# Second attention of a two-layer trunk: its first projections and its first step issued earlier in the program

## The chip, the cores and the metric

The kernel runs on one core of one Trainium2 chip. The metric is the device time of one execution in microseconds (us). A core has five engines that run their own instruction queues in order: PE (TensorE, matrix multiplications and transposes), DVE (VectorE), ACT (ScalarE), POOL (GpSimd) and SP (SyncE, which here issues most of the DMA transfers). [...]

## The reference

Two layers over 1024 tokens of width 1024, each a token mixer and a gated MLP with a causal convolution of width 3. Layer 0 mixes with differential attention (8 heads), layer 1 with multi-head latent attention (16 heads). The change is about the seam between the input of layer 1's mixer and its heads:

```
proj = h @ w_in                                   # 1024 -> 384 + 256 + 32
c_q  = rms_norm(proj[..., :384], q_norm_g)
c_kv = rms_norm(proj[..., 384:640], kv_norm_g)
k_pe = apply_rope(proj[..., 640:], cos, sin)      # one rotary key, shared by all heads
q  = (c_q @ w_uq).reshape(b, s, 16, 64 + 32)      # q_nope, q_pe
kv = (c_kv @ w_ukv).reshape(b, s, 16, 64 + 64)    # k_nope, v
p  = masked_softmax((q_nope . k_nope + q_pe . k_pe) * scale, chunk mask)
out = (p @ v) @ w_o
```

All of it is in float32. A product of two float32 operands is made of three matmuls: each operand is split into a high part and the rest.

## The kernel before

**The latent input** (`mla_input`) loops over `i` = 0 to 9, with eight tiles of 128 tokens (`NT` = 8). Round `i` does `latents(i)` (48 matmuls into one of the two `S` accumulators, then two RMS norms), `turn(i - 1)` (six transposes, then the split into the high and low parts of `c_q` and `c_kv`), and `values(i - 2)` (12 matmuls, two copies by ACT, a DMA of the values to `v_d` in HBM; the first pair's values are also kept on chip by `own`). Round 5 turns the rotary key of tokens 0 to 511 (`rotary(0)`), round 8 that of tokens 512 to 1023 (`rotary(1)`, and `share(1, 1)`, which copies it to the second head's key tile).

**The heads** (`mla_heads`) go in pairs. A pair has six units: `k_unit(p, half)` (6 matmuls, the keys of both heads for one half of the tokens) and `q_unit(h, half)` (9 matmuls). `first()` runs the three units of pair 0 on tokens 0 to 511; before the change it stands in round 7, ahead of `latents(7)`.

**The steps** (`steps`): a head has four steps; each takes two blocks of 128 queries. Step `t` issues `scores(0)` (q times k, row maximum on DVE, exponential on ACT), the units that `units(t)` hands it, the `turn` (transposes of the probabilities, line 252) of step `t - 1`, `weigh(0)`, `scores(1)`, the rest of the units, the `product` with the values (lines 1726 and 1727) of step `t - 1`, and `weigh(1)`. The second attention's steps come in the order p = 1, 0, 3, 2, so its steps 0 and 1 use tokens 0 to 511 alone, and step 2 all of them. Step 0 gets pair 0's three units for tokens 512 to 1023. `prepare(t)` adds fetches and splits of weights and values: in step 0 the fetch of pair 1's weights (`fetch_w(1)`), in step 1 their split, in step 2 the fetch of pair 1's values from `v_d`, in step 4 their split. The differential attention's steps use the same function with its own units of 24 matmuls, into a single accumulator `u`.

**What sets the order.** The kernel says what depends on what; which instruction an engine takes next is fixed when the program is built, by a scheduler that runs through the program with estimated durations and gives each engine the ready instruction that stands first in the program's text order. So a place further up in the text is a higher priority, not a fixed time. Regions under `manual_schedule` keep the order as written; the seam of this change is in none of them. On the chip, every engine then works through its queue in that order.

**The memory** is cut into named places (`s`, `u`, `h` with a number), each used by one tile after another; a ring hands its places out in the order of the calls. `raw` is such a ring of two (`u14`, `u15`): weights from HBM and the values on their way to `v_d` take turns in it. `R.P` is the ring of probability tiles. The eight normalised input tiles of `mla_input` lie in `s4`, `s5`, `s13`, `s0`, `s1`, `s10`, `s11`, `s12`, and each place comes free when `latents` of its tile is done.

Of the kernel before, what the change touches and what calls it, by code (L numbers as in the profile page):

```python
# [17 lines left out]

P = 128
S = 1024  # L20
D = 1024
NT = S // P
KD = D // P
EPS = 1e-6
NEG = -3.0e38

DA_HEADS = 8
# [3 lines left out]
MLA_HEADS = 16  # L31
# [5 lines left out]
FFN = 2816  # L37
NF = FFN // P

# [17 lines left out]
class Trunk:  # L57
# [7 lines left out]
    def __init__(self, tc, ctx, a):  # L65
# [8 lines left out]
        for kind, count, size in (("s", 14, 2048), ("u", 16, 1024), ("h", 14, 512)):  # L74
            for i in range(count):
                self.at(f"{kind}{i}", [P, size])

# [23 lines left out]
    def cut(self, place, size=1024):  # L101

        tile = self.at(place, [P, 2048])
        return [tile[:, i : i + size] for i in range(0, 2048, size)]
# [173 lines left out]
            if n is not None:  # L278
                n -= 1

    def steps(self, attend, units, prepare, n):


        steps = []
        for t in range(n + 2):
            now = before = None
            u = []
            if t < n:
                now = attend(t)
                steps.append(now)  # L290
                prepare(t)
                u = units(t)
                now.scores(0)
            if 0 < t <= n:
                before = steps[t - 1]
            self.run(u, 1)
            if before:
                before.turn()
            if now:
                now.weigh(0)  # L300
                now.scores(1)
            self.run(u)
            if before:
                before.product()
            if now:
                now.weigh(1)
            if t >= 2:
                steps[t - 2].finish()


    def diff_attention(self, o_d, prefetch):
        nc, a = self.nc, self.a
# [5 lines left out]
        R = SimpleNamespace(  # L318
            k=self.ring("u0", "u1", "u2"), qh=self.ring("u3", "u4"), v=self.ring("u5", "u6", "u7"),
            P=self.ring("u8", "u9", "u10", "u11", "u12"), pT=self.ring("u13", "u14", "u15"),  # L320
            o=self.ring("h2", "h3"), fin=self.ring("h4", "h5", "h6", "h7"),
            rope=self.ring("h8", "h9", "h10", "h11"),
        )
# [5 lines left out]
        heads = [dict(q=[None, None], k=[None, None], v=[None, None]) for _ in range(DA_HEADS)]  # L329
# [20 lines left out]
        x, r = [], {}  # L350
# [183 lines left out]
                todo = [[(h, 1, 1)], [(h, 0, 1)], [(h, 2, 1)], []][p]  # L534
            return [unit(*u) for u in todo if u[0] < DA_HEADS]

        self.steps(lambda t: DaStep(self, R, *divmod(t, 4), heads, o_d), units, prepare, 4 * DA_HEADS)

    def da_unit(self, R, H, W, which, half, hd, tab):

# [793 lines left out]
    def mla_input(self, W, hts, turns, v_d, heads_of):  # L1334
# [14 lines left out]
        def latent_tiles(half):  # L1349
            for x, place in zip((cq, ckv), (("s2", "s3"), ("s6", "s7"))[half]):  # L1350
                pieces = self.at(place, [P, 4, 512], F32R)
                for part in range(2):
                    x[part].append(pieces[:, 2 * part : 2 * part + 2, :])
            for part in range(2):
                cq2[part].append(self.at(f"h{2 * half + part}", [P, 512], F32R))
# [7 lines left out]
        def latents(i):  # L1363
            acc = self.big()
            for k in range(KD):
                for b, m, kind in ((0, 384, "q"), (512, 288, "kv")):
                    wh, wl = where[kind, k]
                    self.mm3(acc[:, b : b + m], hts[i][:, 0, k, :], hts[i][:, 1, k, :], wh, wl, k == 0, k == KD - 1)
            nat = nats([P, 672])
            for b, m, off, gain in ((0, 384, 0, g[0]), (512, 256, 384, g[1])):  # L1370
                d = nat[:, off : off + m]
                r = self.rstd(acc[:, b : b + m], d, m)
                nc.vector.scalar_tensor_tensor(d, acc[:, b : b + m], r, gain, ALU.mult, ALU.mult)
            nc.scalar.copy(nat[:, 640:672], acc[:, 768:800])
            return nat

        def turn(i, nat):
            half = i // 4
            s = slice((i % 4) * P, (i % 4 + 1) * P)
            ps = self.bank()  # L1380
            for j in range(3):
                nc.tensor.transpose(ps[:, j * P : (j + 1) * P], nat[:, j * P : (j + 1) * P], self.ident)
            v = ps.rearrange("p (k s) -> p k s", s=P)
            for dst, src in ((cq, v[:, 0:2]), (cq2, v[:, 2])):
                h, l = (x[half][:, s] if dst is cq2 else x[half][:, :, s] for x in dst)
                self.hi(h, src)
                self.lo(l, src, h)
            ps = self.bank()
            for j in range(2):
                nc.tensor.transpose(ps[:, j * P : (j + 1) * P], nat[:, (3 + j) * P : (4 + j) * P], self.ident)  # L1390
            nc.tensor.transpose(ps[:MLA_ROPE, 256:384], nat[:, 640:672], self.ident)
            v = ps[:, :256].rearrange("p (k s) -> p k s", s=P)
            self.hi(ckv[0][half][:, :, s], v)
            self.lo(ckv[1][half][:, :, s], v, ckv[0][half][:, :, s])
            nc.scalar.copy(kp[half][:, s], ps[:MLA_ROPE, 256:384])

        def values(i):
            half = i // 4
            s = slice((i % 4) * P, (i % 4 + 1) * P)
            vs = self.raw([P, D])  # L1400
            for b, y in ((0, self.bank("u")), (512, self.bank())):
                for k in range(2):
                    ch, cl = (cT.kv(part, half, k)[:, s] for part in range(2))
                    self.mm3(y, ch, cl, late.wv[k][0][:, b : b + 512], late.wv[k][1][:, b : b + 512], k == 0, k == 1)
                if b == 0:
                    heads.own(i, y[:, :P])
                nc.scalar.copy(vs[:, b : b + 512], y)
            nc.sync.dma_start(v_d[:, :, i].rearrange("h p e -> p h e"), vs.rearrange("p (h e) -> p h e", e=P))

        def fetch_tab(half):  # L1410
            late.tab = [self.at(place, [MLA_ROPE, 512]) for place in ("h12", "h13")]
            for x in range(2):
                nc.sync.dma_start(late.tab[x], a["rope_k"][:, x, half * 512 : (half + 1) * 512])

        def rotary(half):
            r = self.rope(rope, kp[half], *late.tab, MLA_ROPE // 2, MLA_ROPE)
            t = nats([MLA_ROPE, 2, 512], F32R)
            self.hi(t[:, 0, :], r[:MLA_ROPE])
            self.lo(t[:, 1, :], r[:MLA_ROPE], t[:, 0, :], nc.gpsimd)
            heads.rotary(half, t)  # L1420
# [3 lines left out]
        for i in range(NT + 2):  # L1424
            if readies:
                readies.pop(0)()
            if i == NT - 1:
                heads.share(1, 0)
                heads.first()
            if i < NT:  # L1430
                nat[i] = latents(i)
                if turns:
                    turns.pop(0)()
            if i in (1, 5):
                latent_tiles(i // 4)
            if i == 1:

                late.wv = [self.split(f"s{4 + k}", self.fetch(a["mla_wuv"][k * P : (k + 1) * P, :], D)) for k in range(2)]
                heads = heads_of(cT)
            if i == 4:  # L1440
                fetch_tab(0)
            if 0 <= i - 1 < NT:
                turn(i - 1, nat.pop(i - 1))
            if i >= 2:
                values(i - 2)
            if i == 5:
                rotary(0)
                fetch_tab(1)
            if i == NT:
                rotary(1)  # L1450
                heads.share(1, 1)
        return heads

    def mla_heads(self, cT, v_d, o_d):
        nc, a = self.nc, self.a
        pairs = MLA_HEADS // 2
        heads = [dict() for _ in range(MLA_HEADS)]
        W, V, raws = {}, {}, {}
        w_places = [("u2", "u3"), ("u4", "u5")]
        v_ring, q_ring, t_ring = self.ring("s13", "s4"), self.ring("s1", "s10", "s5", "s9"), self.ring("h10", "h11", "h8")  # L1460
        k_places, kT = ["s0", "s11", "s12", "s8"], []
        cs = self.at("u13", [P, S])
        nc.sync.dma_start(cs, a["rope_q"])
        R = SimpleNamespace(
            P=self.ring("u6", "u7", "u8", "u9", "u12"), pT=self.ring("u0", "u1", "u10", "u11"), o=self.ring("h4", "h5", "h6", "h7"),
        )

        def fetch_w(p):
# [46 lines left out]
        def pair_units(p):  # L1515
            return [
                lambda: k_unit(p, 0), lambda: k_unit(p, 1),
                lambda: q_unit(2 * p, 0), lambda: q_unit(2 * p, 1),
                lambda: q_unit(2 * p + 1, 0), lambda: q_unit(2 * p + 1, 1),
            ]  # L1520
# [1 line left out]
        fetch_w(0)  # L1522
        split_w(0)

        def first():

            self.run([u() for u in pair_units(0)[::2]])

        def own(i, y):

# [49 lines left out]

        prefetch = []

        def rest(step):
            prefetch.append(step)
            self.steps(attend, units, prepare, 4 * MLA_HEADS)

        return SimpleNamespace(first=first, own=own, rotary=rotary, share=share, rest=rest)


class Step:  # L1590
# [431 lines left out]
```

## Time and profile before

| | |
|---|---|
| time, median of 3 runs | 2427.79 us (2427.32 to 2431.45) |
| the profiled execution's own time | 2430.68 us |
| its span from first to last instruction | 2428.9 us |
| PE busy | 2355.0 us of the span |
| DVE, ACT, POOL busy | 1916.0, 1305.3, 618.5 us |
| differential attention, head steps | from about 40 to 510 us |
| latent input | from about 1240 to 1335 us |
| second attention, head steps | from about 1326 to 1680 us |

Engine shares are averages over stages with different limits: the MLP stages (from 620 to 1000 us and from 1820 to 2200 us) have PE busy without a gap. A line such as `1347.25 1.05 ACT L127 CAST s<-u ... [1.46 <-DMA u<-v_d]` in a timeline says: start, duration, engine, line of the kernel, operation, output and input, and in brackets how long the engine had been idle and what it waited for.

### The profile page before, as it was taken

To read this page: it belongs to the slowest core of one execution; us is meant where nothing else is said; L and a number is where in the kernel's file an instruction comes from. 1 tells how busy PE (TensorE), PEld (TensorE's weight loads), DVE (VectorE), ACT (ScalarE), POOL (GpSimd) and SP (SyncE) were. 2 spreads that over 40 slices of the span, in tenths; PEclk is the share of its full clock that TensorE was granted. 3 is DMA by queue.
4 is the path that set the end of the run, shared out by engine and by line. 5 is a ranking of instruction groups with operands and counts; after the bars stand their busy time and mean duration, and the time that the engine had idled before them with its cause. 6 is when DMAs were issued, how large, how long until landed. Compare 5 with 4: busy or idle time off the path is not lost.

```text
span 2428.9 us, 32660 instructions
## 1 busy us (share of the span) xinstructions
PE 2355.0 (97%) x11936; PEld 1997.5 (82%) x11936; DVE 1916.0 (79%) x3111; ACT 1305.3 (54%) x2446; POOL 618.5 (25%) x489
## 2 busy tenths in 40 slices
PE   7999999999999999999999999999999999999998
PEld 6888787887888888878899788988878888887886
DVE  6667776857888888889964777887488888888997
ACT  5677777755444444444445777776244444444444
POOL 4545454424100000000041666665330000000001
PEclk9999999999999999999999999999999999999999
DMA  4111111223322222554221211114322222227502
GB/s 161 40 35 44 35 35 44 100 93 100 99 82 79 87 78 88 187 175 131 72 103 46 77 40 29 49 59 134 96 87 87 79 87 87 78 86 278 172 3 78
DMA packets 95792, 213.91 MB, mean 88 GB/s; under 512 B 8720, under 2 KB 33936, under 8 KB 95632
## 3 DMA queue, kind: packets, MB, share of 16 engines
q1 hardware_dynamic: 86448, 184.04, 23.1%
q10 hardware_dynamic: 9184, 27.79, 3.1%
q8 instruction: 94, 1.54, 0.3%
q14 instruction: 66, 0.54, 0.1%
HBM read 159.37 MB, written 52.43 MB: 87 GB/s over the span
## 4 chain that ended last, share of the span: by engine, by line
PE 82%; DVE 7%; ACT 5%; DMA 3%; issue 2%; POOL 1%; SPq 0%; DVEq 0%; POOLq 0%; ACTq 0%
PE S L119 13%; PE S L121 13%; PE S L120 13%; PE b L119 8%; PE b L120 8%; PE b L121 8%; PE u L119 4%; PE u L120 4%; PE u L121 4%; PE b L252 3%; DMA u<-g_d 2%; PE u L1727 1%; DVE s L130 1%; PE u L1726 1%; ACT s L127 1%
## 5 line engine op out<-in xcount | busy, mean ns | idle before, releaser
L167 POOL TENSOR_TENSOR st<-st,mhalf 128x1 f32<-128x1 f32 x56 | 36.6, 654 | 1314.1 <-DVE st L164 1305.5
L127 ACT CAST u<-h 128x512 fp32r<-128x512 f32 (+2 forms) x242 | 145.9, 619 | 297.4 <-DVE h L847 277.7
L119 PE MATMUL S<-s,u 128*128 128x512 f32 (+1 forms) x768 | 290.5, 378 | 7.6 <-ACT s L127 2.6
L121 PE MATMUL S<-s,u 128*128 128x512 f32 (+1 forms) x768 | 289.5, 377 | 0.1
L120 PE MATMUL S<-s,u 128*128 128x512 f32 (+1 forms) x768 | 289.4, 377 | 0.0
L119 PE MATMUL b<-s,u 128*128 128x512 f32 x588 | 231.0, 393 | 1.5 <-DVE u L130 0.8
L121 PE MATMUL b<-s,u 128*128 128x512 f32 x588 | 229.3, 390 | 0.0
L120 PE MATMUL b<-s,u 128*128 128x512 f32 x588 | 229.2, 390 | 0.0
L904 DVE SCALAR_TENSOR_TENSOR u<-u,conv,u 128x1023 f32<-128x1023 f32 (+1 forms) x176 | 225.8, 1283 | 1.4 <-ACT u L900 1.4
L149 POOL TENSOR_TENSOR u<-u,st 128x384 f32<-128x384 f32 (+7 forms) x160 | 169.7, 1068 | 151.0 <-DVE st L1712 106.7
L127 ACT CAST s<-u 128x512 fp32r<-128x512 f32 (+2 forms) x230 | 145.0, 666 | 108.2 <-PE u L121 35.8
L119 PE MATMUL u<-s,s 128*128 128x512 f32 (+1 forms) x440 | 178.5, 406 | 13.4 <-ACT h L556 7.0
L130 DVE TENSOR_TENSOR u<-b,u 128x512 fp32r<-128x512 f32 (+1 forms) x256 | 157.4, 629 | 29.4 <-ACT u L127 28.0
L119 PEld LDWEIGHTS S<-s,u 128*128 128x128 f32 x768 | 145.2, 189 | 35.1 <-ACT s L127 5.5
L121 PE MATMUL u<-s,s 128*128 128x512 f32 (+1 forms) x440 | 173.2, 394 | 0.0
L120 PE MATMUL u<-s,s 128*128 128x512 f32 (+1 forms) x440 | 172.8, 393 | 0.0
L121 PEld LDWEIGHTS S<-s,u 128*128 128x128 f32 x768 | 145.2, 189 | 26.6 <-DVE u L130 0.5
L120 PEld LDWEIGHTS S<-s,u 128*128 128x128 f32 x768 | 145.3, 189 | 26.1
L130 DVE TENSOR_TENSOR s<-u,s 128x512 fp32r<-128x512 f32 (+2 forms) x210 | 150.0, 746 | 12.4 <-ACT s L127 12.2
L127 ACT CAST u<-b 128x512 fp32r<-128x512 f32 (+1 forms) x256 | 133.2, 550 | 37.9 <-PE b L252 28.9
L907 ACT ACTIVATE u<-u 128x1024 f32<-128x1024 f32 x44 | 46.7, 1062 | 187.5 <-DVE u L904 187.5
L130 DVE TENSOR_TENSOR u<-h,u 128x512 fp32r<-128x512 f32 x164 | 112.7, 687 | 32.5 <-ACT u L127 31.5
(270 smaller groups left out, 6561.1 us busy)
## 6 DMA issues: line engine op xcount, KB each, us to landing
u<-in_ffn_up SPq DMA_DIRECT2D x88, 512.0 KB, 3.9
g_d<-u ACTq DMA_DIRECT2D x44, 512.0 KB, 2.6
u<-in_ffn_down SPq DMA_DIRECT2D x66, 256.0 KB, 4.8
u<-g_d SPq DMA_DIRECT2D x62, 256.0 KB, 4.4
s<-in_da_wqkv SPq DMA_DIRECT2D x23, 512.0 KB, 3.6
x_d<-u SPq DMA_DIRECT2D x16, 512.0 KB, 2.9
s<-x_d SPq DMA_DIRECT2D x8, 1024.0 KB, 10.8
u<-o_d SPq DMA_DIRECT2D x24, 256.0 KB, 2.9
```

The costliest lines, as they stand in the source:

```text
L119: mm(out, lh, rl, start=first, stop=False, skip_group_check=onto)
L120: mm(out, lh, rh, start=False, stop=False, skip_group_check=onto)
L121: mm(out, ll, rh, start=False, stop=last, skip_group_check=onto)
L127: self.nc.scalar.copy(out, src)
L130: (eng or self.nc.vector).tensor_sub(out, src, hi.bitcast(F32))
L149: self.nc.gpsimd.tensor_mul(x, x, s.to_broadcast(list(x.shape)))
L167: nc.gpsimd.tensor_tensor(r, s, self.mhalf, ALU.pow)
L252: self.nc.tensor.transpose(ps[:, j * P : (j + 1) * P], probs[t][:, k : k + P], self.ident)
L904: nc.vector.scalar_tensor_tensor(t[half][:, back:], u[half][:, : S - back], w, t[half][:, back:], ALU.mult, ALU.add)
L907: nc.scalar.activation(t[0], t[0], AF.Silu)
L1726: nc.tensor.matmul(o[:, c0:], v, al, start=kb == 0, stop=False)
L1727: nc.tensor.matmul(o[:, c0:], v, ah, start=False, stop=kb == 2 * p + 1)
```

## The change

- `first` takes the numbers of the units. Keys and the first head's queries of pair 0 (units 0 and 2, tokens 0 to 511) now stand in round 6, ahead of `latents(6)`; the second head's queries (unit 4) stay in round 7.
- `share(1, 0)` moves with them from round 7 to round 6.
- `steps` has become a generator that yields once a step. `early()` issues step 0 of the second attention at the end of round 8, so ahead of `values(7)`, and step 1 at the end of round 9, where it stood before.
- Buffers: the second head's queries go to `s11` and its keys to `s10`, before the other way round; the ring of probabilities starts at `u12` instead of `u6`.
- `steps` gets an option `apart`, set for the differential attention alone: where a step has two units, the first one is issued as a whole, its matmuls ahead of the turn of the step before; before the change its second half came behind `scores(1)`.

```diff
-    def steps(self, attend, units, prepare, n):
+    def steps(self, attend, units, prepare, n, apart=False):
...
-            self.run(u, 1)
+            alone = u[:-1] if apart else []
+            if alone:
+                u = u[-1:]
+            self.run(alone or u, 2 if alone else 1)
             if before:
                 before.turn()
+            self.run(alone)
             if now:
                 now.weigh(0)
                 now.scores(1)
...
+            yield
...
-        self.steps(lambda t: DaStep(self, R, *divmod(t, 4), heads, o_d), units, prepare, 4 * DA_HEADS)
+        self.run([self.steps(lambda t: DaStep(self, R, *divmod(t, 4), heads, o_d), units, prepare, 4 * DA_HEADS, True)])
...
+            if i == NT - 2:
+                heads.share(1, 0)
+                heads.first(0, 2)
             if i == NT - 1:
-                heads.share(1, 0)
-                heads.first()
+                heads.first(4)
...
+            if i >= 8:
+                heads.early()
...
-        v_ring, q_ring, t_ring = self.ring("s13", "s4"), self.ring("s1", "s10", "s5", "s9"), self.ring("h10", "h11", "h8")
-        k_places, kT = ["s0", "s11", "s12", "s8"], []
+        v_ring, q_ring, t_ring = self.ring("s13", "s4"), self.ring("s1", "s11", "s5", "s9"), self.ring("h10", "h11", "h8")
+        k_places, kT = ["s0", "s10", "s12", "s8"], []
...
-            P=self.ring("u6", "u7", "u8", "u9", "u12"), pT=self.ring("u0", "u1", "u10", "u11"), o=self.ring("h4", "h5", "h6", "h7"),
+            P=self.ring("u12", "u6", "u7", "u8", "u9"), pT=self.ring("u0", "u1", "u10", "u11"), o=self.ring("h4", "h5", "h6", "h7"),
...
-        def first():
+        def first(*which):
...
-            self.run([u() for u in pair_units(0)[::2]])
+            self.run([pair_units(0)[x]() for x in which])
...
+        work = [self.steps(attend, units, prepare, 4 * MLA_HEADS)]
+
+        def early():
+            self.run(work, 1)
+
         def rest(step):
             prefetch.append(step)
-            self.steps(attend, units, prepare, 4 * MLA_HEADS)
+            self.run(work)
```

More of the change, by code (lines that the diff above doesn't have):

```diff
@@ L1581, in mla_heads @@
         prefetch = []
+        work = [self.steps(attend, units, prepare, 4 * MLA_HEADS)]
+        def early():
+            self.run(work, 1)
         def rest(step):
             prefetch.append(step)
-            self.steps(attend, units, prepare, 4 * MLA_HEADS)
-        return SimpleNamespace(first=first, own=own, rotary=rotary, share=share, rest=rest)
+            self.run(work)
+        return SimpleNamespace(early=early, first=first, own=own, rotary=rotary, share=share, rest=rest)
 class Step:
```

## The prediction

> **What bounds the kernel now.** I read the first part of the page, then the busy times by stretch, then PE's waits in the stretch of the change, and last the queues of ACT, SP and POOL there.
>
> ```profile
> PE 2355.0 (97%) x11936; PEld 1997.5 (82%) x11936; DVE 1916.0 (79%) x3111; ACT 1305.3 (54%) x2446; POOL 618.5 (25%) x489
> ```
>
> PE is busy for 97% of the span of 2428.9 us. The change adds and removes no matmul, so it can only shift idle time of PE, 73.9 us in all. Where does that lie? The busy times by stretch (columns: PE, PEld, DVE, ACT, POOL, then the granted PE clock) show it for the three stretches that the change touches:
>
> ```profile
> 40.00:510.00 470.00, 448.99 (x2402) 380.96 (x2401) 344.55 (x602) 339.25 (x713) 237.04 (x169) 0.99 0.15 51
> 1300.00:1326.00 26.00, 26.00 (x151) 24.14 (x150) 10.21 (x23) 11.59 (x29) 2.92 (x4) 1.00 0.14 42
> 1326.00:1366.00 40.00, 34.67 (x168) 26.86 (x167) 26.86 (x61) 31.05 (x66) 21.49 (x16) 0.96 0.34 109
> ```
>
> The rounds of the latent input that take up the moved units have no gap at all (26.00 of 26.00). The seam behind them, 1326 to 1366, loses 40.00 - 34.67 = 5.33 us, and runs at a mean clock of 0.96. The differential attention loses 470.00 - 448.99 = 21.0 us. The seam's clock loss sits in one place:
>
> ```profile
> 1354.00:1356.00 2.00, 0.00 (x0) 0.00 (x0) 1.55 (x3) 1.93 (x4) 0.00 (x0) 1.00 0.34 98
> 1356.00:1358.00 2.00, 1.76 (x7) 1.47 (x8) 0.92 (x3) 1.95 (x5) 0.94 (x1) 0.80 0.44 172
> 1358.00:1360.00 2.00, 1.95 (x8) 1.58 (x7) 1.43 (x5) 1.96 (x4) 1.36 (x2) 0.50 0.00 0
> 1360.00:1362.00 2.00, 1.92 (x12) 1.53 (x12) 1.70 (x4) 0.26 (x1) 1.27 (x1) 0.85 0.29 66
> ```
>
> PE stands still for two microseconds, and behind that the clock is 0.80, 0.50 and 0.85. Work lost: 0.20 x 1.76 + 0.50 x 1.95 + 0.15 x 1.92 = 1.6 us. So the seam's ceiling is 5.33 + 1.6 = 6.9 us, 0.28% of the time. What do PE's waits in the seam name?
>
> ```profile
> PE u L1726 <- DVE h L1730: 2.3, 1, 2.3
> PE b L252 <- DVE u L130: 0.9, 1, 0.9
> PE S L119 <- ACT s L127: 0.5, 1, 0.5
> PE b L1382 <- DVE S L1704: 0.5, 1, 0.5
> PE u L1726 <- DVE u L130: 0.4, 1, 0.4
> ```
>
> The 2.3 us is step 1's product, which waits until step 0's has left its accumulator. The 0.5 us of line 119 is step 2's scores, which wait for the second half of the rotary key. Both hang on ACT:
>
> ```profile
> 1342.03 1.05 ACT L127 CAST u<-u 128x1024 fp32r<-128x1024 f32 x1 [1.32 <-DMA u<-in_mla_w]
> 1347.25 1.05 ACT L127 CAST s<-u 128x1024 fp32r<-128x1024 f32 x1 [1.46 <-DMA u<-v_d]
> ...
> 1348.85 1.04 ACT L127 CAST s<-u 32x1024 fp32r<-32x1024 f32 x1
> ...
> 1351.84 2.93 ACT L127 CAST s<-s 64x1024 fp32r<-64x1024 f32 x3
> ...
> 1355.30 0.37 ACT L1729 COPY h<-u 64x256 f32<-64x256 f32 x1
> ```
>
> ACT stood still twice for a DMA, 1.32 us for pair 1's weights and 1.46 us for pair 1's values, though the pair in work needs neither. Then it did the rotary key (1348.85), three copies of it (2.93 us), and only at 1355.30 the copy that frees the accumulator for which PE had waited. So the seam is a queue of ACT that runs late by its two waits for DMA.
>
> **The moved units.** 15 matmuls go from round 7 to round 6. PE has no gap in either round, so they change places with as much other work: zero. Their cover is that full queue. The evictions (DVE and ACT, busy 10.21 and 11.59 of 26.00 us) have room. If the cover were gone, the price would be a wait for the accumulators, at most the 0.9 us of the second wait row above. The exchanged buffers serve this: `s10` is free one round before `s11`. And `u12` is free before `latents(7)` ends, `u6` is not. Neither adds a transfer or a wait, zero too.
>
> **Step 0 ahead of `values(7)`.** Three units (6 + 9 + 9 = 24 matmuls) change places with 12 matmuls. The pace of full-width matmuls:
>
> ```profile
> 1700.00:1720.00 20.00, 20.00 (x90) 16.57 (x89) 4.64 (x4) 2.49 (x4) 4.34 (x4) 1.00 0.18 53
> ```
>
> 20.00 / 90 = 0.22 us each, so the units come 12 x 0.22 = 2.7 us sooner, and `values(7)` 24 x 0.22 = 5.3 us later at most. PE is full in this part, which by itself is zero again. The step's DMA counts too. SP's queue:
>
> ```profile
> 1331.19 0.36 SPq L1408 DMA_DIRECT2D v_d<-u  x1
> 1335.13 0.36 SPq L1408 DMA_DIRECT2D v_d<-u  x1
> 1338.36 0.35 SPq L135 DMA_DIRECT2D u<-in_mla_w  x1
> 1339.92 0.36 SPq L1408 DMA_DIRECT2D v_d<-u  x1
> 1343.94 0.34 SPq L135 DMA_DIRECT2D u<-v_d  x1
> ```
> ```profile
> v_d<-u SPq DMA_DIRECT2D x6, 512.0 KB, 3.2
> u<-in_mla_w SPq DMA_DIRECT2D x3, 512.0 KB, 3.6
> ```
>
> The rows at 1331.19, 1335.13 and 1339.92 are the stores of `values(5)`, `(6)` and `(7)`. `fetch_w(1)` takes the next place of the `raw` ring. Today that is the one of `values(6)`, so it waits for that store to land (1335.13 + 3.2 = 1338.3, and it goes at 1338.36). Ahead of `values(7)` in the text it gets the place of `values(5)`, whose store lands at 1331.19 + 3.2 = 1334.4, so it goes behind the next store, at about 1335.5: 2.9 us sooner. The weights land at 1339.1 instead of 1342.0. That takes away ACT's wait of 1.32 us, and lets POOL begin earlier:
>
> ```profile
> 1343.16 2.39 POOL L130 TENSOR_TENSOR u<-u,u 128x1024 fp32r<-128x1024 f32 x1 [1.62 <-ACT u L127]
> ...
> 1346.53 1.28 POOL L130 TENSOR_TENSOR u<-h,u 32x512 fp32r<-32x512 f32 x1
> ```
>
> The second row is the low part of the rotary key, behind the weights' low part. POOL's idle 1.62 us ahead of them goes, and the rotary key with its copies comes between 1.3 and 2.9 us sooner. I take 2.3: the fetch is what both queues waited for, which speaks for a value nearer to its own 2.9. Thereby the three copies lie where ACT was idle, the copy at 1355.30 comes at 1353.0, and the 2.3 us wait closes.
>
> **The sum for the seam.** Gone: 0.5 us (step 2's scores), 0.4 us (the first product), 2.3 us, and with the pause the clock's 1.6 us. That is 4.8 us. What is late next: the wait of 0.9 us at step 2's turn and the 0.5 us behind `latents(7)` stay. `values(7)` is later, so ACT waits for `v_d` somewhere else in its queue; I leave that wait at its 1.46 us, bounded by 0 below and 1.46 + 5.3 us above. Both ends stay in the range. I subtract 0.2 us for the part of a pause that stays: 4.6 us.
>
> The clock is the part that I am least sure of. [...]
>
> **The differential attention.** `apart` moves 12 matmuls of a step's first unit ahead of the previous step's turn and of `scores(1)`, in 14 of 32 steps. Do these ever part the unit today?
>
> ```profile
> 61.74 0.49 PE L252 MATMUL b<-ident,u 128*128 128x128 f32 x3
> 61.98 0.48 PE L119 MATMUL u<-s,s 128*128 128x512 f32 x1
> ```
>
> Here, in the first head, yes: 12 matmuls, three transposes, 12 matmuls. In the later heads that I followed, the first unit runs ahead of them as a whole, since the previous step's probabilities are not ready yet. And the waits there have other releasers:
>
> ```profile
> PE u L119 <- ACT h L556: 7.0, 6, 1.3
> ...
> PE u L119 <- DVE h L238: 3.4, 5, 1.4
> ```
>
> The 7.0 us is for a value unit to leave `u`, which `apart` doesn't touch. The 3.4 us is for a key or query unit to leave it; this is what an earlier end of the first unit could shorten. At most 3.4 us gained; as much lost if turns come 12 x 0.22 = 2.7 us late and products wait for them. I take zero, nearest to the row at 61.74, where only three short transposes move.
>
> **The time.** The profiled execution took 2430.68 us, 2.89 above the median of 2427.79. From 2430.68, 4.6 less is 2426.1; on the median's scale 2427.79 - 4.6 = 2423.2, or -0.19%. About 0.2%, 4.9 us, is what a measurement of this kernel can tell from no change, and the forecast lies just at that line.
>
> **The rivals.**
>
> *The seam keeps its waits (about 2427.5).* ACT's queue has 31.05 us of work in 40.00 us, and what is taken out at 1342 may come back behind it, as the three copies and the exponentials follow at once. For it: ACT is busy 1.93 of 2.00 us in the very pause of PE. Against it: in the same 40 us it is idle for 8.95 us, 2.78 of them in the two waits for DMA.
>
> *Slower: ACT stuck behind the later values (2432.6).* One chain ends in ACT's second wait:
>
> ```profile
> 1339.92 3.97 DMA v_d<-u
> 1343.94 3.29 DMA u<-v_d
> 1347.25 1.57 ACT s L127 x2
> ```
>
> The last row is the split of pair 1's values, first needed in step 8. If `values(7)` moves back by 5.3 us but this split keeps its place ahead of the rotary key's copies, ACT starts it at 1352.6, and all behind it on ACT (copies, exponentials, the copy that frees the product's accumulator) comes 5.3 us late. The other half of the change gives ACT 1.3 us at most against that; the longer pause may cost the clock's 1.6 us once more, of which I take half, 0.8: 5.3 - 1.3 + 0.8 = +4.8 us. It decides once the split stands more than 1.3 us too early for its data. Against it: the order of the queue is made anew, and the scheduler sees `values(7)` late as well, so it should set the split back too; only its error in the DMA time (the 1.46 us) should stay.
>
> *POOL and DVE meet (2425.0).* In the seam a DVE subtraction of usual length 0.79 us took 2.47 us while POOL ran:
>
> ```profile
> 1348.38 2.39 POOL L130 TENSOR_TENSOR s<-u,s 128x1024 fp32r<-128x1024 f32 x1 [0.57 <-ACT s L127]
> 1345.30 0.79 DVE L130 TENSOR_TENSOR s<-h,s 128x512 fp32r<-128x512 f32 x1
> 1348.85 2.47 DVE L130 TENSOR_TENSOR s<-h,s 128x512 fp32r<-128x512 f32 x1 [0.32 <-ACT s L127]
> ```
>
> DVE ended at 1351.32, just behind POOL's 1350.77. POOL's work on the weights now falls on step 0's query splits, the same instruction, and may stretch another one by 2.47 - 0.79 = 1.7 us: 1.7 us of the gain lost, 2423.2 + 1.7 = 2424.9, about 2425.0. [...]
>
> *The differential attention moves by itself.* Its order is made anew too: 3.4 us either way by the rows above, 7 us if a pause of the clock's kind appears or goes.
>
> **How the numbers follow.** The seam closes as forecast (gain between 3.2 and 6.9 us, with the POOL case in it): 0.55, of which 0.32 beyond 0.2% and 0.23 within. It keeps its waits: 0.20 (0.03 faster, 0.14 the same, 0.03 slower, by the other attention). ACT stuck: 0.12 (0.02 the same, 0.10 slower). The differential attention decides: 0.13 (0.07 faster, 0.06 slower). Faster 0.42, the same 0.39, slower 0.19. Range: below, the seam's ceiling with 3.4 us from the differential attention, 2427.79 - 10.3 = 2417.5; above, no gain in the seam and 3.4 us lost, 2431.2. The stuck case beyond that is the part left out.
>
> **What would show it.** Right: in the stretch 1326 to 1366 PE above 38 of 40 us and clock 0.99 or more; `fetch_w(1)` ahead of the last store in SP's queue, and no ACT wait for it; no wait of line 1726 above 1 us; 40 to 510 within 3 us of 448.99. Wrong: a wait of ACT for `v_d` above 3 us, a stretched DVE subtraction on step 0's queries, or a changed sum in the differential attention, larger than the seam's.

## The result and the profile after

The changed kernel takes 2426.25 us (median of 20 runs, 2422.26 to 2429.82), the kernel before 2429.93 us on the same chip (20 runs, 2425.95 to 2432.05): a ratio of 0.9985, 95% interval [0.9978, 0.9991], or 3.7 us less. A second timing gave 0.9982 [0.9972, 0.9992]. So the size is about what was forecast. Where the time is won is not where it was forecast.

The first part of the page of the changed kernel (span 2424.7 us):

```profile
PE 2351.8 (97%) x11936; PEld 1995.3 (82%) x11936; DVE 1910.7 (79%) x3111; ACT 1306.9 (54%) x2446; POOL 618.6 (26%) x489
```

Its busy times by stretch, the same columns as in the prediction (PE, PEld, DVE, ACT, POOL, granted PE clock, then the DMA engines' share and GB/s):

```profile
40.00:510.00 470.00, 450.91 (x2422) 381.88 (x2421) 340.51 (x602) 339.44 (x713) 236.51 (x169) 1.00 0.16 51
1300.00:1326.00 26.00, 26.00 (x152) 24.13 (x151) 10.01 (x23) 11.71 (x29) 2.93 (x4) 1.00 0.14 42
1326.00:1366.00 40.00, 34.66 (x173) 27.76 (x172) 27.35 (x67) 32.12 (x70) 22.68 (x17) 0.96 0.36 109
1420.00:1512.00 92.00, 92.00 (x606) 83.28 (x605) 74.40 (x183) 70.94 (x154) 61.93 (x49) 1.00 0.13 37
```

The seam, 1326 to 1366, has not gained at all: PE idle 40.00 - 34.66 = 5.34 us (5.33 before), clock 0.96 as before. The last row is a stretch that the prediction never looked at, steps 14 to 31 of the second attention by their exponentials. PE is now busy in it without a gap. The same stretch of the kernel before:

```profile
1420.00:1512.00 92.00, 89.52 (x581) 79.89 (x580) 72.67 (x178) 66.54 (x148) 60.44 (x47) 1.00 0.13 37
```

There PE stood idle for 2.48 us. Why did the seam not gain? PE's waits there in the changed kernel, but for two of 0.2 us that were there before:

```profile
PE S L119 <- ACT u L1719: 4.2, 4, 1.4
PE b L1386 <- DVE S L1717: 0.5, 1, 0.5
PE b L119 <- DVE s L130: 0.2, 1, 0.2
```

(Lines are 4 to 13 higher than before: 1719 is the exponential, 1739 and 1740 the product.) The wait of the product (2.3 us), that of step 2's scores for the rotary key (0.5), and those of 0.9 and 0.4 us are all gone. In their place the scores wait four times, 4.2 us in all, for an exponential of ACT to empty one of the two `S` accumulators. The queues of SP and ACT show what happened to the steps of the forecast:

```profile
1334.18 0.35 SPq L135 DMA_DIRECT2D u<-in_mla_w  x1
1346.38 0.36 SPq L1412 DMA_DIRECT2D v_d<-u  x1
1349.87 0.34 SPq L135 DMA_DIRECT2D u<-v_d  x1
```
```profile
1338.18 1.05 ACT L127 CAST u<-u 128x1024 fp32r<-128x1024 f32 x1 [1.30 <-DMA u<-in_mla_w]
...
1346.86 1.05 ACT L127 CAST s<-u 32x1024 fp32r<-32x1024 f32 x1
...
1348.43 2.94 ACT L127 CAST s<-s 64x1024 fp32r<-64x1024 f32 x3
...
1352.37 0.37 ACT L1742 COPY h<-u 64x256 f32<-64x256 f32 x1
1352.77 1.01 ACT L1719 ACTIVATE u<-S,st 128x896 f32<-128x896 f32 x1
...
1353.76 1.04 ACT L127 CAST s<-u 128x1024 fp32r<-128x1024 f32 x1
```

The weights are fetched 4.2 us sooner than before (1334.18 against 1338.36; the forecast was 1335.5). ACT still stands 1.30 us for them, since its cast moved up in the queue by 3.85 us too. The rotary key's cast comes 2.0 us sooner, its copies 3.4, the copy that frees the product's accumulator 2.9. The last row, the split of pair 1's values, comes 6.5 us later and waits for nothing.

**Where the 3.7 us went.** Between the first store to `v_d` and the 14th of the 32 stores to `o_d` both kernels do the same number of instructions on PE, DVE, ACT and POOL, and behind it PE's order is the same. The busy times of these two stretches, before and after:

```profile
1271.00:1510.32 239.32, 231.29 (x1410) 204.92 (x1409) 162.12 (x388) 158.53 (x360) 123.21 (x102) 0.99 0.17 50
```
```profile
1270.70:1506.31 235.61, 229.30 (x1410) 205.22 (x1409) 161.33 (x388) 159.77 (x360) 123.32 (x102) 0.99 0.18 51
```

239.32 - 235.61 = 3.71 us less for equal work (239.35 and 235.60 from the first store's exact start, as in the table below): 1.72 us of idle time (8.03 against 6.31) and 1.99 us of busy time. The idle part is the sum of -2.48 us in 1420 to 1512 and +0.75 in 1366 to 1420; the seam is level. The waits that are gone behind the seam, before (1400 to 1512), and the only one there after:

```profile
PE b L252 <- DVE u L130: 1.0, 2, 0.8
PE S L119 <- ACT u L1706: 0.7, 2, 0.5
PE b L119 <- DVE u L130: 0.4, 1, 0.4
PE b L252 <- DVE S L1704: 0.3, 1, 0.3
```
```profile
PE b L119 <- DVE u L130: 0.3, 1, 0.3
```

PE's transposes (line 252) waited for DVE, and the scores for ACT. At the longest of these waits (0.80 us at 1431.43) DVE had two row maxima of 0.94 and 0.56 us ahead of the split at 1430.70; in the changed kernel's order a split stands ahead of such a row maximum (0.69 us at 1430.16). The busy part lies in many small differences of the mean duration (the product's matmuls, 283 against 281 ns, the scores' lines 120 and 121, 352 against 349 ns); I have not found its cause.

### The profile page after: what moved, and what is told of

It is laid out like the page before. It is cut to its first block, busy times and chain, and to the rows that moved or that the text cites. A ratio compares the mean times of both kernels' runs of the same rounds, so it can differ in the third digit from the quotient of the medians.

```text
span 2424.7 us, 32649 instructions
## 1 busy us (share of the span) xinstructions
PE 2351.8 (97%) x11936; PEld 1995.3 (82%) x11936; DVE 1910.7 (79%) x3111; ACT 1306.9 (54%) x2446; POOL 618.6 (26%) x489
## 4 chain that ended last, share of the span: by engine, by line
PE 83%; DVE 6%; ACT 4%; DMA 3%; issue 2%; POOL 1%; SPq 0%; POOLq 0%; DVEq 0%; ACTq 0%
PE S L119 13%; PE S L121 13%; PE S L120 13%; PE b L119 8%; PE b L120 8%; PE b L121 8%; PE u L119 4%; PE u L120 4%; PE u L121 4%; PE b L252 3%; PE u L1740 1%; PE u L1739 1%; DMA u<-g_d 1%; DVE s L130 1%; ACT s L127 1%
## 5 line engine op out<-in xcount | busy, mean ns | idle before, releaser
L127 ACT CAST s<-u 128x512 fp32r<-128x512 f32 (+3 forms) x230 | 144.9, 665 | 115.8 <-PE u L121 37.2
L127 ACT CAST s<-h 128x512 fp32r<-128x512 f32 x128 | 77.3, 619 | 115.7 <-DVE h L1083 61.8
```

The source lines that it names most:

```text
L127: self.nc.scalar.copy(out, src)
```

## The experiments

The measure used beside the time is this stretch, first store to `v_d` to 14th store to `o_d`, in each profile. From the 14th to the last store every kernel but one took 186.0 to 187.1 us.

| kernel | ratio to before | stretch, us | PE idle in it | PE clock in the seam |
|---|---|---|---|---|
| before | | 239.35 | 8.03 | 0.96 |
| e1_apart | 0.9998 [0.9990, 1.0007] | 239.56 | 8.67 | 0.96 |
| e3_first | 1.0009 [1.0000, 1.0018] | 239.67 | 8.61 | 0.96 |
| e10_fetch | 1.0006 [0.9997, 1.0015] | 240.20 | 9.20 | 0.91 |
| e11_units | 1.0005 [0.9996, 1.0013] | 238.69 | 7.49 | 0.96 |
| e5_latefetch | 1.0032 [1.0020, 1.0044] | 240.19, then 195.05 | 8.99 | 0.91 |
| e2_seam | 1.0001 [0.9991, 1.0010] | 234.51 | 6.80 | 1.00 |
| e4_early | 0.9990 [0.9981, 1.0000] | 235.63 | 5.14 | 0.91 |
| the change | 0.9985 [0.9978, 0.9991] | 235.60 | 6.31 | 0.96 |
| c1_after (again) | 0.9982 [0.9972, 0.9992] | 235.53 | 6.31 | 0.96 |
| e8_pool | 1.0009 [0.9999, 1.0020] | 240.53 | 8.52 | 0.91 |
| e13_wpool | 0.9990 [0.9981, 0.9998] | 238.30 | 7.36 | 0.94 |
| e12_units | 0.9978 [0.9968, 0.9989] | 233.96 | 5.98 | 1.00 |
| e14_units | 0.9980 [0.9970, 0.9990] | 234.10 | 5.36 | 0.96 |

**The parts: e1_apart, e2_seam, e3_first, e4_early, c1_after.** e1 is the kernel before with the option of the differential attention alone:

```diff
-        self.steps(lambda t: DaStep(...), units, prepare, 4 * DA_HEADS)
+        self.run([self.steps(lambda t: DaStep(...), units, prepare, 4 * DA_HEADS, True)])
```

> The kernel before with only the option apart in the differential attention. Theory now (from the trace after): the differential attention itself gives about 3 us, so the first fetch of ffn_up goes near 567.4 instead of 570.4 us in the profile, and the time is about 3 us below the kernel before, less what the transfer-bound down projection (1004 to 1060 us) takes back or not from run to run; the second attention is unchanged, its last o_d store 1697 less the same shift. Rival (the prediction's): the option is worth nothing, 0 within 1 us, and the 3 us is the scatter of one profile.

e2 is the whole change but for that `True`.

> Everything of the change except the option apart. Theory now: the gain of about 4 us arises in the second attention but behind the seam (steps 8 and later, 1430 to 1512 us); PE's idle time in 1326 to 1366 stays near 5.3 us, the first ffn_up fetch near 570.4, the last o_d store about 4 us nearer to the first v_d store than before (426.2 us apart before, 421.8 after). The prediction's theory: the seam itself closes, PE above 38 of 40 us there.

e3 has only the first projections and their buffers (units 0 and 2 and `share(1, 0)` in round 6, unit 4 in round 7, `s10` and `s11` exchanged; no `early`, no `apart`).

> Only the earlier first projections (rounds 6 and 7), with share(1, 0) and the exchanged s10 and s11; no early step, no apart, ring of probabilities as before. Both theories: 0 within 1 us, since PE is full in these rounds. A rival that credits the earlier projections: up to 2 us faster.

e4 has only the early step, with the projections in round 7 and the buffers as before:

```diff
+            if i >= 8:
+                heads.early()
```

> Only the early step 0 (at the end of round 8, ahead of values(7)); projections, buffers and differential attention as before. Theory now: this alone carries the second attention's gain, about 4 us between the first v_d store and the last o_d store (422 instead of 426.2 us). Rival: it needs the earlier projections and the exchanged buffers, and gives less than 1.5 us alone.

c1 is the change once more.

> The whole change once more, on the same chip as the next three. If the first result holds: ratio 0.9985, about 3.5 us faster, from the first v_d store to the last o_d store about 422 us (426.2 before). If apart matters beside the early step: faster than the early step alone was (0.999). Rival: it is the early step alone, and then 0.999 here too.

Alone, the projections and buffers are worth nothing (1.0009, stretch 239.67), nor is `apart` (0.9998). e1's stretch bears that out, but its first fetch of the MLP came at 569.9 us in the profile, not near the 567.4 that were expected. The early step alone has the change's stretch (235.63, no idle time of PE in 1420 to 1512) and a ratio of 0.9990, whose interval ends at 1.0000. In its profile the seam's idle time did fall, to 3.72 us, but its clock fell too, to 0.91. e2 has the short stretch too (234.51), but its time, 1.0001, doesn't show it: its runs had a mean granted clock of 0.9947, those of before beside it 0.9962. What a thousandth of clock costs is told at the end; by that, some 2 us of e2's gain are covered. Whether `apart` adds something to the early step, the timings don't settle.

**What of the early step: e10_fetch and e5_latefetch.** The early step does two things: pair 1's weights are fetched sooner, and the units and scores stand ahead of `values(7)`. e10 does the first alone, in the kernel before:

```diff
             if i == NT:
                 rotary(1)
                 heads.share(1, 1)
+                heads.fetch()
...
-            if t == 0:
-                fetch_w(1)
```

> The kernel before with one edit: the fetch of pair 1's weights ahead of values(7), so about 3 us sooner; the steps stay where they were. The prediction's theory: rotary key and accumulator copy come 1.3 to 2.9 us sooner, PE's wait of 2.3 us at 1354 closes, 2 to 4 us faster. Theory now: the order of the queues hardly changes, ACT and PE wait for the next thing, 0 within 1.5 us.

e5 does the second alone (e4 with the fetch in step 1):

```diff
-            if t == 0:
-                fetch_w(1)
             if t == 1:
+                fetch_w(1)
                 split_w(1)
```

> Step 0 early as in the early-step kernel, but the fetch of pair 1's weights stays behind the store of values(7), in step 1. If the early fetch carries the gain: 0 within 1 us, 426 us from the first v_d store to the last o_d store. If the order of units and values carries it: about 422.5 us there, about 3 us faster in all. The prediction put the gain on the fetch (ACT's 1.3 us and POOL's 1.6 us).

PE's waits in e10's seam, and in e5 behind it (1420 to 1690):

```profile
PE u L1725 <- DVE h L1729: 4.4, 1, 4.4
PE S L119 <- ACT u L1705: 0.8, 1, 0.8
```
```profile
PE b L252 <- DVE u L130: 4.8, 9, 0.9
PE S L119 <- ACT u L1716: 2.1, 1, 2.1
```

Neither half carries the gain. With the fetch alone PE's waits of 0.9, 0.5 and 0.4 us are gone and it comes to the product 1.9 us sooner, counted from the first store to `v_d`. But ACT's copy that frees the accumulator is no sooner (84.55 us behind that store, 84.33 before), as ACT still waits 1.21 us for the weights, and 1.79 us for pair 1's values. So the product's wait is longer than before, 4.4 us. With the units alone the order behind the seam is another one: turns wait nine times, the rest behind the 14th store takes 195.05 instead of 186 us, and the kernel loses 8 us, which neither of the two expectations had. So the place of one 512 KB fetch decides over 10 us (0.9990 against 1.0032); in the profiles 4.6 us of it lie ahead of the 14th store (240.19 against 235.63) and 8.0 behind it (195.05 against 187.09), far from the seam.

**Is the new wait ACT's queue? e8_pool and e13_wpool.** Between the exponentials ACT has casts. e8 is the change with the second halves of two rotary key copies on POOL, which stands idle for 6.80 us there:

```diff
-            self.hi(kT[j][64:128, :, s], kT[0][64:128, :, s])
+            if j > 1 and half:
+                nc.gpsimd.tensor_copy(kT[j][64:128, :, s], kT[0][64:128, :, s])
+            else:
+                self.hi(kT[j][64:128, :, s], kT[0][64:128, :, s])
```

> The changed kernel, with the copies of the rotary key's second half for the third and fourth key tile on POOL instead of ACT (about 2 us less on ACT in the seam, where POOL was idle for 6.8 us). If the seam after the change is bound by ACT's exponentials coming late (PE waited 4.2 us there for line 1719): these waits shrink to 2 to 3 us, and the time falls by 1 to 3 us against the changed kernel. Rival: the softmax chain itself (DVE maximum, exponential, scale on POOL) sets the pace: waits stay above 3.5 us, 0 within 1 us, or slower as POOL now scales later.

e13 is the change with the cast of pair 2's weights there:

```diff
-            self.hi(W[p][0], raw)
+            if p == 2:
+                nc.gpsimd.tensor_copy(W[p][0], raw)
+            else:
+                self.hi(W[p][0], raw)
```

> The whole change, with the cast of pair 2's weights (1.05 us of ACT in the seam, at 1356.28) moved to POOL, which stands idle for 6.8 us there. If the scores wait for their accumulators because ACT's queue holds casts between the exponentials, 1.05 us goes out of it, the waits of the scores in the seam fall from 4.2 to about 3.2 us, and the time by 1 us: ratio to before about 0.998. Rival: the chain maximum, exponential, next scores sets the pace by itself, and the waits stay at 4 us or turn into others; then the time is that of the change or, since the order is remade, up to 5 us worse (as with the rotary key's copies on POOL, 1.0009).

PE's longest waits in the seam of e8, then of e13:

```profile
PE S L119 <- ACT u L1722: 4.2, 4, 1.5
PE u L1742 <- DVE h L1746: 1.2, 1, 1.2
```
```profile
PE S L119 <- ACT u L1722: 5.0, 6, 1.4
```

2 us and 1 us less work on ACT, and the scores wait 4.2 and 5.0 us: the sum of the waits doesn't fall. That doesn't clear ACT's queue, though. In the changed kernel ACT has no wait from 1344.29 to 1360.7 us, and the four exponentials start 1.5, 2.5, 2.0 and 0.8 us after DVE has their row maximum ready: they stand behind other work of ACT. In e13 the wait right behind the moved cast does fall, from 1.42 to 0.47 us, by about the cast's length; the next one grows from 0.61 to 1.40 us, and there ACT stands idle for 0.59 us until a row maximum is ready. In e8 the queue is another one: ACT waits 1.46 us for pair 1's values again, just ahead of the first of these exponentials. So ACT's queue is what is late in the changed kernel, and close behind it comes the chain of the rival, row maximum, exponential and next scores through two accumulators. That this chain sets the pace by itself is not shown. e8 loses all of the gain (1.0009). Of e13 the stretch is 2.7 us longer than the change's, but the intervals of the two ratios overlap.

**Is it the order behind the seam by itself? e11_units, e12_units, e14_units.** In the kernel before, e11 puts pair 1's units sooner. It was meant to leave every queue as it is through the seam; in the trace PE's order is the same up to the pause of 2.3 us, and behind that (from 1356 us on) nine matmuls of a unit come first:

```diff
-            at = (2, 3, 4, 5, 6, 7) if p == 0 else (0, 1, 3, 4, 5, 7)
+            at = (2, 2, 3, 4, 5, 7) if p == 0 else (0, 1, 3, 4, 5, 7)
```

> The kernel before, with two of pair 1's units one step sooner: its second key unit in step 2 instead of 3, its first query units in steps 3 and 4 instead of 4 and 5, and the next in step 5 instead of 6. Every engine's queue is as before up to and through the seam; only the order of some 150 of PE's rows behind it (steps 2 to 6) differs. Theory A (the whole gain of the change comes from the order in which the queues run through steps 2 to 12, which the early step only happens to remake): this edit remakes that order too, so the time of the second attention should move by more than 2 us, either way, with the seam's idle time at 5.3 us as before. Theory B (the early step itself carries the gain, by what it brings forward; the order behind it is neutral): 0 +- 1 us.

e12 is the change with the same edit.

> The whole change, with the same shift of pair 1's units. Theory A: the gain over the kernel before is not kept as it is; the second attention lies more than 2 us from the 421.8 us of the change, and the difference between this kernel and the same shift without the change isn't 4 us. Theory B: it is faster than the same shift without the change by 3.5 to 4.5 us (ratio about 0.9984), as the change is than the kernel before.

e11 is level with before (1.0005, the waits of 1420 to 1512 unchanged at 2.48 us). e12 is the fastest kernel of the study: 2424.56 us, 0.9978. So theory A fails for this edit, and of theory B the direction holds: the early step brings its gain in both orders, 239.35 - 235.60 = 3.8 us of the stretch without the shift and 238.69 - 233.96 = 4.7 us with it. By the times the difference between e11 and e12 is 7.3 us, more than the 3.5 to 4.5 us of theory B; their mean granted clocks, 0.9952 and 0.9970, can account for 2.7 us of that (last section). The 2.48 us of waits at 1420 to 1512 stand in before, e1, e3, e10, e11 and e5 (2.48 to 2.74 us), and are 0.01 us at most in the change, c1, e2, e4, e12, e13 and e14. Only e8, where they are 1.82 us, has the early step with its fetch and keeps most of them.

In e12's seam PE waits for less:

```profile
PE S L119 <- ACT u L1719: 1.6, 2, 1.4
PE b L252 <- DVE s L130: 0.9, 1, 0.9
```

Two units in step 2 give PE work while the exponentials empty the accumulators. e14 asked whether a unit in step 1 does it better still:

```diff
-            at = (2, 3, 4, 5, 6, 7) if p == 0 else (0, 1, 3, 4, 5, 7)
+            at = (1, 2, 3, 4, 5, 7) if p == 0 else (0, 1, 3, 4, 5, 7)
```

> The whole change, with five of pair 1's six units one step sooner: one in each of the steps 1 to 5, the last in step 7 as before. With two of them in step 2 the scores' wait for their accumulators fell from 4.2 to 1.6 us. If that is because PE had other work to do while the exponentials emptied the accumulators (theory), a unit in step 1, before the first of these waits (1.39 us), takes part of that one away too: waits of the scores below 1.6 us, the second attention at 420 us or less, ratio to before 0.9975 to 0.998. Rival: the shift of the units only remade the order, and the place of the filler doesn't matter; then the scores' waits are anywhere from 1.6 to 4.2 us, and the time is that of the change, 0.9983 to 0.999.

```profile
PE u L1739 <- DVE u L130: 2.7, 1, 2.7
PE b L1386 <- DVE S L1717: 0.5, 1, 0.5
PE S L119 <- ACT u L1719: 0.4, 1, 0.4
```

The scores' waits all but close, as expected, and the product waits 2.7 us in their place, now for a turn's split. Idle time of the seam: 4.37 us, e12 4.06, the change 5.34. By their ratios both lie below the change, but the intervals overlap, and some 1.5 us of e12's lead over the kernel before may be clock (0.9970 against 0.9960). That e12 and e14 beat the change is not shown by the times; their stretches are 1.6 and 1.5 us shorter than its own.

## Why the prediction was right in the sum and wrong in the place

**The time.** Forecast -0.19%, measured -0.15% [-0.22, -0.09]. That they agree is luck: the seam, to which the whole forecast was put, gave nothing, and no term stands for the place that gave 3.7 us.

**The moved units and the buffers: zero.** Right (e3: 1.0009, stretch 239.67 against 239.35).

**Step 0 ahead of `values(7)`.** The mechanics came as worked out: fetch at 1334.18 (forecast 1335.5), rotary key 2.0 us sooner (2.3), the copy at 1352.37 (1353.0), the product's wait of 2.3 us gone, and no ACT stuck behind the later values (no wait at 1353.76). One detail was wrong: ACT's wait for the weights didn't go, because the cast moved up with the fetch. And while POOL worked on the rotary key (1344.99, 1.28 us) a split of DVE took 1.35 us at 1345.46, against 0.69 for one of the same shape at 1342.05: not the 1.7 us more of the rival.

**The sum for the seam: 4.6 us.** This is the step that failed. The waits of 0.5, 0.4 and 2.3 us were taken off, and beyond them 0.9 us closed that was left standing, but nothing was put in their place. "What is late next" was looked for in two waits that were there already and in ACT's DMA waits. Next were the exponentials that empty the two `S` accumulators, 4.2 us. For the seam, the rival "the seam keeps its waits" was the true one, and for its reason: what was taken out of ACT's queue came back behind it, and the exponentials stood there late. What the rival didn't say is that a row maximum stands next behind them (e13).

**The gain behind the seam.** No term of the prediction stands for it. It was in reach: the trace of before shows 2.48 us of PE's idle time in 1420 to 1512, with six small waits, and the text itself said that the queues' order is made anew. That a part of the program whose text doesn't change gets another order, and gains or loses more than the edited part (-2.5 us of idle time here, +9 us of length in e5), was given a chance for the differential attention only. Why the early fetch and the early units together lead to the order without these waits is not explained by these runs; that they do so is shown by the table.

**The clock: 1.6 us.** The closed pause gave none back; 0.96 before and after. Behind the pause of 2.28 us the clock was 0.80, 0.50 and 0.85; four shorter pauses, of 0.61 to 1.42 us, took its place, and behind them it was 0.64 and 0.51: see the last section. (Without this term the sum is 4.6 - 1.6 = 3.0 us.) No run shows the 3.2 us at which the forecast's range of gains begins, the three waits without the clock: the seam's idle time was 5.33 us before and 5.34 after.

**The differential attention: zero.** The timing agrees (e1, 0.9998 [0.9990, 1.0007]). The trace moves more than that: the first fetch of the MLP behind it goes at 567.39 instead of 570.37 us, 3.0 us sooner, and the first store to `v_d` at 1270.71 instead of 1270.97. The early part of it is clock. Before, and after, behind the waits at the last heads:

```profile
448.00:450.00 2.00, 0.86 (x4) 0.38 (x2) 2.00 (x3) 0.79 (x2) 1.26 (x1) 0.81 0.74 272
450.00:452.00 2.00, 1.70 (x4) 1.42 (x5) 1.97 (x6) 2.00 (x5) 1.28 (x1) 0.50 0.70 240
452.00:454.00 2.00, 2.00 (x6) 1.52 (x6) 1.97 (x3) 1.95 (x4) 0.00 (x0) 0.50 0.01 2
454.00:456.00 2.00, 2.00 (x6) 1.53 (x5) 1.36 (x3) 0.94 (x4) 0.00 (x0) 0.50 0.00 0
```
```profile
450.00:452.00 2.00, 2.00 (x20) 2.00 (x19) 1.97 (x2) 1.60 (x3) 0.72 (x1) 1.00 0.01 2
452.00:454.00 2.00, 2.00 (x12) 1.70 (x12) 1.98 (x7) 1.48 (x5) 1.35 (x1) 1.00 0.00 0
```

The kernel before loses 0.19 x 0.86 + 0.50 x (1.70 + 2.00 + 2.00) = 3.0 us of work there. All seven profiles without `apart` have a clock of 0.86 to 0.93 in 440 to 464, all seven with it 1.00. The first fetch of the MLP comes at 571.2 us on the mean of the seven without it and at 568.5 us on that of the seven with it. So `apart` does do something. In the changed kernel the gain was then given back in the down projection of the MLP, where a wait grew from 2.13 to 2.94 us, at a time when the DMA engines' share was 1.00 (1044 to 1048 us), and the clock behind it was 0.50 and 0.66 (1050 to 1054), 1.00 before. From the first fetch of the MLP to the first store to `v_d` the change, c1 and e12 take 703.1 to 703.5 us; the other four profiles with `apart`, and all without it, take 699.3 to 701.0. The seven come to `v_d` at 1270.0 us on the mean, those without it at 1271.2. Between nothing and some 2 us is therefore what `apart` may be worth, and the prediction's bound of 3.4 us held. Its reason did not quite: the 7.0 us of waits for value units, "which `apart` doesn't touch", fell to 4.2, beside the 3.4 us that it might shorten, which fell to 2.3 (waits from 80 to 510 us; counted from 40 us on, these last are 4.5 us before and after).

## What to carry to other kernels

When a wait of the busiest engine is taken away, write down what that engine will wait for next at the very same place, resource by resource (here two accumulators), before counting the wait as gain. Where a scheduler orders the queues, an edit in the text's order remakes the order far behind the edit: compare a stretch of equal work (same instruction counts, ending where the orders agree again) rather than the edited stretch, and expect a size of several microseconds of either sign. Try the part that moves against each of its halves: here two halves that are worth nothing and -8 us make +4 us together.

## What the runs showed of the hardware that was not expected

**The clock falls at a few places, and not every time.** Summed over stretches of 4 us, (1 - clock) x PE's busy time is 4.5 us in the changed kernel's profile, 5.8 in before's, 9.2 in e2's and 10.6 in e11's. In the ten profiles read in such stretches it falls by more than a trace, up to 2400 us, at the same seven places (48, 448, 600, 1045, 1357, 1785 and 2228 us, within some 10 us), in each profile at some of them. e5 has a loss where no other profile has one: its mean clock from 1510.2 to 1704.4 us is 0.99, in the others' matching stretches 1.00. The pauses by themselves don't decide it. The changed kernel and e2 have the same waits of the scores, one microsecond apart in time; the rows of the changed kernel, then of e2:

```profile
1353.92 0.50 PE L119 MATMUL S<-s,s 128*128 128x512 f32 x1 [1.39 <-ACT u L1719]
1356.43 0.50 PE L119 MATMUL S<-s,s 128*128 128x512 f32 x1 [0.81 <-ACT u L1719]
1359.16 0.44 PE L119 MATMUL S<-s,s 128*128 128x384 f32 x1 [1.42 <-ACT u L1719]
1360.79 0.80 PE L119 MATMUL S<-s,s 128*128 128x512 f32 x1 [0.61 <-ACT u L1719]
```
```profile
1354.91 0.50 PE L119 MATMUL S<-s,s 128*128 128x512 f32 x1 [1.40 <-ACT u L1719]
1357.43 0.50 PE L119 MATMUL S<-s,s 128*128 128x512 f32 x1 [0.81 <-ACT u L1719]
1360.16 0.44 PE L119 MATMUL S<-s,s 128*128 128x384 f32 x1 [1.41 <-ACT u L1719]
1361.79 0.50 PE L119 MATMUL S<-s,s 128*128 128x512 f32 x1 [0.62 <-ACT u L1719]
```

Their clock in the 4 us behind, the changed kernel, then e2:

```profile
1360.00:1362.00 2.00, 1.39 (x5) 1.03 (x4) 1.60 (x6) 0.97 (x3) 2.00 (x2) 0.64 0.29 68
1362.00:1364.00 2.00, 2.00 (x11) 1.80 (x10) 0.93 (x4) 1.05 (x4) 2.00 (x2) 0.51 0.00 0
```
```profile
1360.00:1362.00 2.00, 1.23 (x6) 0.96 (x7) 1.93 (x6) 1.69 (x5) 2.00 (x2) 1.00 0.43 172
1362.00:1364.00 2.00, 2.00 (x16) 1.81 (x15) 1.57 (x7) 1.23 (x4) 2.00 (x1) 1.00 0.29 66
```

Equal pauses, one with half the clock behind them and one without; these rows don't show what decides it. In the work from the first store to `v_d` to the 14th to `o_d`, e2's PE is busy for 227.7 us and the changed kernel's for 229.3, so this one fall (a mean clock of 0.51 from 1360.50 to 1363.90 us) cost some 1.6 us of PE's time.

**The scatter of the times is largely this clock.** Over 129 executions of the twelve experiments' kernels, within each kernel, the time falls by 1.50 +- 0.14 us for every 0.001 of mean granted clock, and with that taken out the scatter of one execution falls from 2.1 to 1.5 us. A kernel whose runs happened to have 0.0015 less clock, as e2's did, looks 2.3 us slower. Whether its own pauses brought that clock, these runs can't tell.
